# An FFN square and a gated residual computed in place in PSUM, and low words of weights stored one block earlier

## The chip, the core and the metric

The kernel runs on one core of a Trainium2 chip. Five engines matter: TensorE (PE in the profile, PEld for its weight loads), VectorE (DVE), ScalarE (ACT), GpSimd (POOL) and SyncE (SP), which only issues DMAs. The metric is the device time of one execution in microseconds; the kernel before takes 3242.33 us, the median of three runs (3240.86 to 3249.45).

## The reference

One layer of an encoder: 2048 prompt rows (16 tiles of 128) and 8 x 16 sample rows (one tile, SMP) go through a modulated norm, an input projection, two mixers (a gated delta rule and a band attention), an output projection with a gated residual, and an FFN with a squared relu and a second gated residual. The part that the change touches:

```python
    x = x + g1 * (jnp.concatenate([o_a, o_b], axis=-1) @ w_out)
    h = rmsnorm(x, norm2_g) * (1 + sc2) + sh2
    x = x + g2 * (jnp.square(jax.nn.relu(h @ w_up)) @ w_down)
```

Here w_out is 1024 x 1024, w_up 1024 x 4096 and w_down 4096 x 1024, all in float32.

## The kernel before

All large products are taken in three matmuls on split operands: an operand is rounded to a high word (type fp32r), and the remainder is a low word. `mm3` (L160) issues high x high, high x low and low x high into one PSUM accumulation.

Weights arrive in pieces of 128 x 1024 through `weights` (L166). SyncE loads the piece into a buffer `raw` (3 of them, `self.nraw`), ScalarE casts it into the high half of a buffer `w` (4 of them, `self.nw`), and the low half comes in one of two ways. If the low word of this piece was stored in DRAM earlier, SyncE loads it from there (L178). If not, GpSimd subtracts the high half from raw (L180) and, where `self.keep[name]` is set, SyncE stores the low half for later blocks (L183). All these DMAs stand in SyncE's one queue, in order.

Phase 1 (up to about 1127 us) is norm, input projection and the mixer of group A. Phase 2 goes over the blocks of tiles `BLOCKS2` = [0, 1], [2..5], [6..9], [10..13], [14, 15, SMP]. The text calls them blocks 0 to 4. For each block, `out_proj` (L1429) multiplies by w_out (8 pieces), applies gate and residual and prepares the norm, and `ffn` (L1492) multiplies by w_up (32 pieces, one `psu` each) and w_down (32 pieces). After each four rows of w_up, w_down's two halves follow for each tile (`psd`), and the next w_up piece is already issued in between. Attention for the next block is cut into steps and mixed into the FFN by a pace (`tick`). The final order of the instructions on each engine is the scheduler's, which runs when the program is built.

All of this shares one PSUM pool of `GP` = 3 banks (tag "g"): psu, psd, pso and the transposes for the norm. A bank comes free after the last reader. In `ffn_up` ScalarE writes the relu to `r` (one buffer) and its square, rounded, to the high word of `u`. VectorE squares r in place and subtracts the high word, which makes the low word of u. In `out_proj` VectorE writes the gated product to `gt` and adds it to `x1`. In block 0 the three weights are not kept, in block 1 all three are, and blocks 2 to 4 load all low words.

Of the kernel before, what the change touches and what calls it, by code (L numbers as in the profile page):

```python
# [8 lines left out]
F32 = mybir.dt.float32  # L9
F32R = mybir.dt.float32r  # L10
AF = mybir.ActivationFunctionType
ALU = mybir.AluOpType
AX = mybir.AxisListType.X

P = 128
# [36 lines left out]
class Trunk:  # L52
# [1376 lines left out]
    def out_proj(self, tiles, gates):  # L1429

        nc = self.nc
        x1 = []
        for j, t in enumerate(tiles):
            cs = slice(j * P, (j + 1) * P)
            for q, src in enumerate((self.s_oa, self.s_ob)):
                f = self.hp.tile([P, 4, P], F32, tag="htmp", name="of", bufs=2)
                nc.sync.dma_start(f, src[t])
                ks = slice(4 * q, 4 * q + 4)
                self.split(self.hT[:, ks, 0, cs], self.hT[:, ks, 1, cs], f)
        sts = [self.small.tile([P, 2, 6], F32, tag="bst", name="ost", bufs=NT2) for _ in tiles]  # L1440
        for group in ((0,), (1,), (2, 3)):
            wq = [self.wslices("w_out", 0, q * 256, 256, KT, 4) for q in group]
            for j, t in enumerate(tiles):
                if group[0] == 0:
                    x = self.fp.tile([P, D], F32, tag="x1", name="x1", bufs=self.nt)
                    nc.sync.dma_start(x, self.x_src(t))
                    x1.append(x)
                cs = slice(j * P, (j + 1) * P)
                for q, ws in zip(group, wq):
                    hs = slice(q * 256, (q + 1) * 256)  # L1450
                    ps = self.gp.tile([P, 512], F32, tag="g", name="pso")[:, 0:256]
                    for k in range(KT):
                        self.mm3(ps, self.hT[:, k, 0, cs], self.hT[:, k, 1, cs], ws[k][0], ws[k][1], k == 0, k == KT - 1)
                    tm = self.fp.tile([P, 256], F32, tag="gt", name="gt", bufs=2)
                    self.tt(tm, ps, gates[j][:, hs], ALU.mult)
                    self.tt(x1[j][:, hs], x1[j][:, hs], tm, ALU.add)
                    if q % 2:
                        nc.vector.bn_stats(sts[j][:, q // 2], x1[j][:, (q // 2) * 512:(q // 2 + 1) * 512])
                    self.tick(24 * 256)
                if group[-1] == 3:  # L1460
                    xn = self.normed(x1[j], t, sts[j])
                    self.later(lambda j=j, t=t, xn=xn: self.load_b(j, self.load_a(t, xn, 2, 3)), 3)
        return x1
# [6 lines left out]
    def ffn_up(self, fi, h2, T):  # L1470
        nc = self.nc
        mm = nc.tensor.matmul
        ws = self.wslices("w_up", 0, fi * P, P, KT, KT)
        ps = self.gp.tile([P, 512], F32, tag="g", name="psu")
        for c0, c1 in (((0, 256), (256, T)) if fi == 0 and T == 512 else ((0, T),)):
            if c1 == T:
                self.flush()
            for k in range(KT):
                wh, wl = ws[k]
                mm(ps[:, c0:c1], wh, h2[:, k, 0, c0:c1], start=(k == 0), stop=False)  # L1480
                mm(ps[:, c0:c1], wh, h2[:, k, 1, c0:c1], start=False, stop=False)  # L1481
                mm(ps[:, c0:c1], wl, h2[:, k, 0, c0:c1], start=False, stop=(k == KT - 1))  # L1482
        r = self.fp.tile([P, self.nt * P], F32, tag="r", name="r", bufs=1)
        self.act(r[:, 0:T], ps[:, 0:T], AF.Relu)
        u = self.fp.tile([P, 2, self.nt * P], F32R, tag="u", name="u", bufs=NGRP + 1)
        self.act(u[:, 0, 0:T], r[:, 0:T], AF.Square)
        self.tt(r[:, 0:T], r[:, 0:T], r[:, 0:T], ALU.mult)
        self.tt(u[:, 1, 0:T], r[:, 0:T], u[:, 0, 0:T].bitcast(F32), ALU.subtract)
        self.tick(24 * T)
        return u  # L1490

# [36 lines left out]
    def phase2(self):  # L1528
        nc, tc = self.nc, self.tc
        with ExitStack() as st:  # L1530
            P_ = lambda name, **kw: st.enter_context(tc.tile_pool(name=name, bufs=1, **kw))
            self.p2, self.hp, self.fp, self.sp = (P_(x) for x in ("p2c", "p2h", "p2f", "p2s"))
            self.nt = NT2
            self.xnp, self.xntag, self.nxn, self.inplace = self.fp, "y", self.nt, False
            self.hT = self.p2.tile([P, KT, 2, self.nt * P], F32R, name="hT2")
            for bi, tiles in enumerate(BLOCKS2):
                n = len(tiles)
                self.keep.update({k: bi == 1 for k in ("w_out", "w_up", "w_down")})
                gates = {t == SMP: None for t in tiles}
                for k in gates:  # L1540
                    gates[k] = self.gate_tile(0, k)
                x1 = self.out_proj(tiles, [gates[t == SMP] for t in tiles])
                if bi + 1 < len(BLOCKS2):
                    self.queue(*self.attention(BLOCKS2[bi + 1]))
                    if SMP in BLOCKS2[bi + 1]:
                        self.queue(self.sample_gen(), 2 + 9 * NB)
                    self.pace(0.95 * n * 24 * 2 * FF)
                self.ffn(tiles, self.hT, x1)
# [43 lines left out]
```

## Time and profile before

| what | value |
|---|---|
| median of three runs | 3242.33 us |
| profiled execution, its own time | 3235.24 us |
| its span from first to last instruction | 3233.5 us |
| PE busy | 3071.4 us, 95% of the span |
| VectorE, ScalarE, GpSimd busy | 59%, 46%, 22% |
| mean granted clock of TensorE | 0.977 |
| DMA | 730.71 MB, 226 GB/s over the span |

A matmul's end is modelled and matmuls overlap, so the busy time of PE says where it had work and not how fast it was. [...] By the instructions' tiles, the projection of block 0 begins at 1127 us and its FFN at 1187, the projection of block 1 at 1439 and its FFN at 1535, block 2 at 1941.

### The profile page before, as it was taken

Reading aid. Unit: us, or ns where it says so; the run is one execution under the profiler, and the core shown is the slowest. Engines: PE = TensorE matmul, PEld = TensorE weight load, DVE = VectorE, ACT = ScalarE, POOL = GpSimd, SP = SyncE. Lnnn points to the kernel's source line nnn. Section 1 sums busy time; section 2 is a strip of 40 time slices with the busy share of each in tenths; the row PEclk is TensorE's granted clock in tenths of the full one; section 3 lists DMA queues with packets and bytes.
Section 4 is the critical chain, followed back from the end, with each engine's and each line's share of the span. In section 5 each row is a group of like instructions: output and inputs, shape, how many; then the busy total and the mean of one; then the engine's idle time right before and its main releaser. Section 6 shows DMA issues by size and latency. Waiting matters only on the chain.

```text
span 3233.5 us, 53068 instructions
## 1 busy us (share of the span) xinstructions
PE 3071.4 (95%) x19577; PEld 2713.0 (84%) x19577; DVE 1903.2 (59%) x4526; ACT 1478.5 (46%) x2707; POOL 701.2 (22%) x561
## 2 busy tenths in 40 slices
PE   7899999999999979988999999999999999998998
PEld 6798988899989968878888889888888887787997
DVE  5985777777868676888446567235455443243223
ACT  3554544556656555554424444344434443333332
POOL 4641312121222347653343320000000000000000
PEclk9999999999989999998999999999999999998999
DMA  9789896878888765565565666665676667677875
GB/s 298 225 264 283 269 288 207 266 236 245 282 292 262 223 201 167 160 222 174 170 200 188 204 214 228 195 195 186 204 246 191 209 230 230 222 239 224 258 246 195
DMA packets 624507, 730.71 MB, mean 226 GB/s; under 512 B 59040, under 2 KB 483088, under 8 KB 622200
## 3 DMA queue, kind: packets, MB, share of 16 engines
q1 hardware_dynamic: 618488, 695.87, 68.0%
q0 software_dynamic: 5760, 31.46, 3.0%
q8 instruction: 154, 2.52, 0.3%
q14 instruction: 105, 0.86, 0.1%
HBM read 614.57 MB, written 115.52 MB: 226 GB/s over the span
## 4 chain that ended last, share of the span: by engine, by line
PE 71%; DVE 12%; DMA 9%; issue 3%; ACT 2%; SPq 1%; POOL 1%; POOLq 0%; DVEq 0%; ACTq 0%
PE psd L164 7%; PE psd L162 7%; PE psu L1480 7%; PE psu L1481 7%; PE psd L163 7%; PE psu L1482 7%; PE pv L1285 2%; PE psq L521 2%; PE psq L520 2%; PE psq L519 2%; PE psb L162 2%; PE psb L164 2%; PE psb L163 2%; PE psS L1267 2%; PE pso L162 2%
## 5 line engine op out<-in xcount | busy, mean ns | idle before, releaser
L175 ACT CAST w<-raw 128x1024 fp32r<-128x1024 f32 (+1 forms) x528 | 552.7, 1048 | 349.2 <-PE psd L164 163.2
L82 POOL TENSOR_TENSOR w<-raw,w 128x1024 fp32r<-128x1024 f32 (+1 forms) x172 | 418.3, 2443 | 365.8 <-ACT w L175 327.5
L1480 PE MATMUL psu<-hT,w 128*128 128x512 f32 (+2 forms) x1304 | 468.6, 361 | 7.1 <-ACT hT L104 6.2
L1481 PE MATMUL psu<-hT,w 128*128 128x512 f32 (+2 forms) x1304 | 467.2, 359 | 1.2 <-DVE hT L82 1.2
L1482 PE MATMUL psu<-hT,w 128*128 128x512 f32 (+2 forms) x1304 | 465.7, 357 | 0.0
L164 PE MATMUL psd<-w,u 128*128 128x512 f32 x1088 | 431.4, 398 | 9.1 <-DVE u L82 9.1
L162 PE MATMUL psd<-w,u 128*128 128x512 f32 x1088 | 432.5, 398 | 7.9 <-DVE y L82 4.1
L163 PE MATMUL psd<-w,u 128*128 128x512 f32 x1088 | 427.6, 393 | 0.0
L82 DVE TENSOR_TENSOR r<-r 128x512 f32<-128x512 f32 (+2 forms) x160 | 178.8, 1117 | 399.7 <-ACT u L92 399.4
L82 DVE TENSOR_TENSOR y<-y,psd 128x512 f32<-128x512 f32 x238 | 162.2, 684 | 242.0 <-PE psd L164 241.4
L1480 PEld LDWEIGHTS psu<-hT,w 128*128 128x128 f32 x1304 | 246.6, 190 | 39.8 <-ACT hT L104 7.4
L1481 PEld LDWEIGHTS psu<-hT,w 128*128 128x128 f32 x1304 | 246.8, 189 | 33.2 <-DVE hT L82 2.3
L1482 PEld LDWEIGHTS psu<-hT,w 128*128 128x128 f32 x1304 | 246.6, 189 | 32.5 <-issue 0.2
L92 ACT ACTIVATE r<-psu 128x512 f32<-128x512 f32 (+2 forms) x160 | 85.5, 534 | 408.7 <-PE psu L1482 349.6
L164 PEld LDWEIGHTS psd<-w,u 128*128 128x128 f32 x1088 | 204.9, 189 | 56.7 <-DVE u L82 10.4
L162 PEld LDWEIGHTS psd<-w,u 128*128 128x128 f32 x1088 | 205.3, 189 | 53.5 <-DVE y L82 6.7
L163 PEld LDWEIGHTS psd<-w,u 128*128 128x128 f32 x1088 | 205.6, 189 | 45.4 <-issue 1.0
L162 PE MATMUL psb<-w,hT 128*128 128x256 f32 x816 | 236.3, 290 | 0.7 <-ACT qraw L976 0.7
L164 PE MATMUL psb<-w,hT 128*128 128x256 f32 x816 | 234.1, 288 | 0.5 <-DVE hT L82 0.5
L163 PE MATMUL psb<-w,hT 128*128 128x256 f32 x816 | 233.4, 287 | 0.0
L520 PE MATMUL psq<-hT,w 128*128 128x384 f32 (+1 forms) x576 | 194.1, 337 | 0.0
L521 PE MATMUL psq<-hT,w 128*128 128x384 f32 (+1 forms) x576 | 193.9, 337 | 0.0
(318 smaller groups left out, 6603.0 us busy)
## 6 DMA issues: line engine op xcount, KB each, us to landing
raw<-in_w_up_dram SPq DMA_DIRECT2D x160, 512.0 KB
raw<-in_w_down_dram SPq DMA_DIRECT2D x160, 512.0 KB
raw<-in_w_in_dram SPq DMA_DIRECT2D x156, 512.0 KB
w<-s_w_in SPq DMA_DIRECT2D x130, 512.0 KB
w<-s_w_up SPq DMA_DIRECT2D x96, 512.0 KB
w<-s_w_down SPq DMA_DIRECT2D x96, 512.0 KB
raw<-in_w_out_dram SPq DMA_DIRECT2D x40, 512.0 KB
x<-in_x_prompt_dram SPq DMA_DIRECT2D x38, 512.0 KB
```

What stands on the lines that cost most here:

```text
L82: (eng or self.nc.vector).tensor_tensor(out, in0, in1, op)
L92: self.nc.scalar.activation(out, in_, func, **kw)
L162: mm(out, lh, rh, start=first, stop=False)
L163: mm(out, lh, rl, start=False, stop=False)
L164: mm(out, ll, rh, start=False, stop=last)
L175: nc.scalar.copy(w[:, 0, 0:n], r)
L519: mm(ps[:, 0:T], wh, hT[:, k, 0, 0:T], start=(k == 0), stop=False)
L520: mm(ps[:, 0:T], wh, hT[:, k, 1, 0:T], start=False, stop=False)
L521: mm(ps[:, 0:T], wl, hT[:, k, 0, 0:T], start=False, stop=(k == KT - 1))
L1480: mm(ps[:, c0:c1], wh, h2[:, k, 0, c0:c1], start=(k == 0), stop=False)
L1481: mm(ps[:, c0:c1], wh, h2[:, k, 1, c0:c1], start=False, stop=False)
L1482: mm(ps[:, c0:c1], wl, h2[:, k, 0, c0:c1], start=False, stop=(k == KT - 1))
```

## The change

There are three edits. In `out_proj` the product with the gate is written back into the PSUM bank and x1 is added from there; the buffer gt is gone. In `ffn_up` VectorE forms max(psu, 0) times r, which is the square, in the PSUM bank, and the low word is taken from the bank; r is no longer written by VectorE. In `phase2` the low words of w_out and w_down are made and stored in block 0 and loaded from block 1 on; those of w_up are made in blocks 0 and 1, stored in block 1 and loaded from block 2 on.

```diff
-                    tm = self.fp.tile([P, 256], F32, tag="gt", name="gt", bufs=2)
-                    self.tt(tm, ps, gates[j][:, hs], ALU.mult)
-                    self.tt(x1[j][:, hs], x1[j][:, hs], tm, ALU.add)
+                    self.tt(ps, ps, gates[j][:, hs], ALU.mult)
+                    self.tt(x1[j][:, hs], ps, x1[j][:, hs], ALU.add)
...
-        self.tt(r[:, 0:T], r[:, 0:T], r[:, 0:T], ALU.mult)
-        self.tt(u[:, 1, 0:T], r[:, 0:T], u[:, 0, 0:T].bitcast(F32), ALU.subtract)
+        self.stt(ps[:, 0:T], ps[:, 0:T], 0.0, r[:, 0:T], ALU.max, ALU.mult)
+        self.tt(u[:, 1, 0:T], ps[:, 0:T], u[:, 0, 0:T].bitcast(F32), ALU.subtract)
...
-                self.keep.update({k: bi == 1 for k in ("w_out", "w_up", "w_down")})
+                self.keep.update(w_out=bi == 0, w_up=bi == 1, w_down=bi == 0)
```

The scheduler also puts the instructions of phase 2 in another order; PE's order is the same up to the first projection of block 0. On VectorE, in the second group of w_up pieces of block 0's FFN (numbers tell the buffers apart: r and u are the relu and the two words of the square, psu the bank), there stood:

```order
L82 TENSOR_TENSOR r_15516<-r_15516 128x256
L82 TENSOR_TENSOR u_15518<-r_15516,u_15518 128x256
L82 TENSOR_TENSOR r_15562<-r_15562 128x256
L82 TENSOR_TENSOR u_15564<-r_15562,u_15564 128x256
L82 TENSOR_TENSOR r_15608<-r_15608 128x256
```

and now there stands:

```order
L79 SCALAR_TENSOR_TENSOR psu_15495<-psu_15495,r_15520 128x256
L82 TENSOR_TENSOR u_15522<-psu_15495,u_15522 128x256
L79 SCALAR_TENSOR_TENSOR psu_15541<-psu_15541,r_15566 128x256
L82 TENSOR_TENSOR u_15568<-psu_15541,u_15568 128x256
L79 SCALAR_TENSOR_TENSOR psu_15587<-psu_15587,r_15612 128x256
```

The number of VectorE's instructions is the same; both of each pair now read the bank, and only the first of them reads r.

On SyncE, at the first pieces of w_down in block 0 (raw and w are the buffers of a piece, s_w_down the stored low words, s_ob attention's output, q its queries), there stood:

```order
L174 DMA raw_15442<-in_w_down_dram 128x2x512
L174 DMA raw_15447<-in_w_down_dram 128x2x512
L1240 DMA q_16516<-s_q 128x128
L174 DMA raw_15487<-in_w_up_dram 128x8x128
L174 DMA raw_15533<-in_w_up_dram 128x8x128
```

and now there stands:

```order
L174 DMA raw_15444<-in_w_down_dram 128x2x512
L1292 DMA s_ob<-of_16025 64x128
L183 DMA s_w_down<-w_15391 128x1024
L174 DMA raw_15450<-in_w_down_dram 128x2x512
L1240 DMA q_16528<-s_q 128x128
L183 DMA s_w_down<-w_15397 128x1024
L174 DMA raw_15491<-in_w_up_dram 128x8x128
L183 DMA s_w_down<-w_15443 128x1024
L174 DMA raw_15537<-in_w_up_dram 128x8x128
```

Each store of a low word stands just ahead of the load of the raw piece that comes three pieces later, which takes the raw buffer of the piece stored.

## Rows read from the trace of the kernel before

**Rows 1.** Windows: stretch, length, busy us (instructions) per engine, clock, DMA share, GB/s
```profile
core 0: us, PE busy (x) PEld busy (x) DVE busy (x) ACT busy (x) POOL busy (x), PEclk, DMA share, GB/s
0.00:1120.00 1120.00, 1049.24 (x8241) 970.08 (x8242) 828.78 (x2482) 593.83 (x1238) 313.96 (x302) 0.97 0.83 260
...
1127.00:1187.00 60.00, 44.66 (x295) 40.34 (x296) 40.39 (x98) 30.03 (x58) 26.99 (x24) 0.86 0.71 232
1187.00:1439.00 252.00, 227.12 (x1467) 202.19 (x1466) 200.08 (x295) 137.99 (x252) 157.77 (x81) 0.98 0.56 169
1439.00:1535.00 96.00, 79.38 (x574) 75.64 (x573) 79.42 (x166) 42.86 (x82) 29.56 (x22) 0.86 0.61 197
1535.00:1941.00 406.00, 403.51 (x1960) 336.03 (x1958) 221.52 (x348) 167.05 (x274) 149.93 (x79) 1.00 0.61 195
1941.00:2413.00 472.00, 466.95 (x2480) 399.20 (x2481) 224.03 (x491) 202.74 (x336) 10.17 (x28) 1.00 0.63 205
```

**Rows 2.** Waits of PE in 1187:1439: us in total, times, longest us
```profile
PE psd L164 <- DVE u L82: 9.1, 3, 3.6
PE psd L162 <- ACT r L92: 3.7, 2, 2.6
PE psS L1267 <- DVE sm L1113: 2.8, 3, 1.2
...
PE psu L1480 <- ACT r L92: 0.9, 1, 0.9
```

**Rows 3.** Lines in 1187:1439: group xcount | busy us, mean ns | idle before, releasers
```profile
L82 POOL TENSOR_TENSOR w<-raw,w 128x1024 fp32r<-128x1024 f32 x63 | 154.8, 2472 | 76.9 <-ACT w L175 73.0 <-DMA raw<-in_w_out_dram 2.6 <-POOL bias L1235 0.8
L175 ACT CAST w<-raw 128x1024 fp32r<-128x1024 f32 x64 | 66.7, 1046 | 22.9 <-DMA raw<-in_w_down_dram 7.4 <-PE psd L164 7.1 <-DMA raw<-in_w_up_dram 3.0
L82 DVE TENSOR_TENSOR r<-r 128x256 f32<-128x256 f32 x32 | 51.5, 1609 | 29.5 <-ACT u L92 29.5
L82 DVE TENSOR_TENSOR u<-r,u 128x256 fp32r<-128x256 f32 x32 | 41.9, 1309 | 1.1
...
L92 ACT ACTIVATE u<-r 128x256 fp32r<-128x256 f32 x32 | 13.4, 418 | 0.3
L92 ACT ACTIVATE r<-psu 128x256 f32<-128x256 f32 x32 | 12.3, 385 | 50.4 <-DVE u L82 41.4 <-PE psu L1482 4.6 <-DVE sm L1116 4.2
```

**Rows 4.** Timeline in 1208:1214: start us, us, instruction, idle before and releaser
```profile
1205.71 4.87 POOL L82 TENSOR_TENSOR w<-raw,w 128x1024 fp32r<-128x1024 f32 x2 [3.08 <-ACT w L175]
1205.97 2.40 DVE L82 TENSOR_TENSOR r<-r 128x256 f32<-128x256 f32 x1 [0.44 <-ACT u L92]
...
1211.75 0.43 DVE L82 TENSOR_TENSOR r<-r 128x256 f32<-128x256 f32 x1 [0.90 <-ACT u L92]
```

**Rows 5.** Lines of VectorE in 1127:1187
```profile
L82 DVE TENSOR_TENSOR x<-x,gt 128x256 f32<-128x256 f32 x8 | 7.7, 983 | 0.1
L82 DVE TENSOR_TENSOR gt<-pso,gate 128x256 f32<-128x256 f32 x8 | 3.1, 414 | 0.7 <-PE pso L164 0.4 <-DMA x<-in_x_prompt_dram 0.3
```

**Rows 6.** Windows of PE alone: psu and psd of 512 columns, psu of 256
```profile
1550.00:1630.00 80.00, 80.00 (x350) 1.00 0.58 181
1225.00:1235.00 10.00, 10.00 (x86) 1.00 0.49 141
```

**Rows 7.** Waits of SyncE's queue in 1187:1439
```profile
SPq L174 <- POOL w L82: 90.2, 38, 5.6
```

**Rows 8.** Waits of PE in 1439:1535
```profile
PE pv L1285 <- DVE PT L82: 5.2, 2, 4.6
```

**Rows 9.** Lines in 1941:2413, block 2
```profile
L82 DVE TENSOR_TENSOR y<-y,psd 128x512 f32<-128x512 f32 x57 | 38.9, 686 | 59.0 <-PE psd L164 58.8
L82 DVE TENSOR_TENSOR r<-r 128x512 f32<-128x512 f32 x32 | 22.0, 688 | 89.3 <-ACT u L92 89.1
...
L92 ACT ACTIVATE r<-psu 128x512 f32<-128x512 f32 x32 | 19.2, 599 | 89.7 <-PE psu L1482 89.7
```

## The prediction

> **What bounds the kernel now.** I read the windows by stage first, since block by block the work differs. [rows 1] has PE busy for nearly all of each FFN stage from block 1 on: 403.5 of 406 us in 1535:1941, 467.0 of 472 in 1941:2413. There the matmuls set the time and an edit on VectorE can only cost. Three stretches are different: the projection of block 0 (1127:1187, PE idle 60 - 44.7 = 15.3 us), the FFN of block 0 (1187:1439, idle 252 - 227.1 = 24.9) and the projection of block 1 (1439:1535, idle 96 - 79.4 = 16.6). They are also where the granted clock is not full: 0.86, 0.98, 0.86. All that the change can give lies in these 408 us.
>
> Next, who is late there. In block 0's FFN the waits of PE [rows 2] name the square chain: psd on the low word u 9.1 us, psd on r 3.7 and psu on r 0.9, together 13.7 of 24.9; after that VectorE's softmax maximum with 2.8. Then why it is late [rows 3]: r times r takes 1609 ns on average for 256 columns and the low word 1309, and ScalarE's relu stood idle 41.4 us until VectorE had finished with the one buffer r. The timeline shows the reason [rows 4]: with GpSimd in two low words of weights (4.87 us in a row) r times r takes 2.40 us; a few microseconds later, the same shape takes 0.43. An operation that reads one operand from PSUM is not slowed beside the same GpSimd work: gt from pso and gate takes 414 ns in the stretch where x plus gt, both in SBUF, takes 983 [rows 5].
>
> **The change part by part.** *The square in the bank.* Both operations of the chain now have one operand in PSUM. A write of VectorE into PSUM stands nowhere in this trace, so I bound it: at best the 414 ns of [rows 5], at worst the 1609 ns of the operation that it replaces [rows 3]. I take 414, since the shape, the engine and the PSUM read are the same. Then VectorE loses 32 x (1.609 - 0.414) + 32 x (1.309 - 0.414) = 38 + 29 = 67 us of its 200 in block 0. The loop through r falls from 0.385 + 0.418 + 1.609 + 1.309 = 3.7 us to 0.385 + 0.418 = 0.8 us until r is free, since the square on ScalarE and the new multiply run side by side, and 1.2 us until u is done. One group of 24 matmuls of 256 columns takes 24 x 10.0/86 = 2.8 us [rows 6]: before, the loop was the slower of the two, afterwards it is not. So the 13.7 us go. [...] Of the 2.8 us on the softmax I give back 1.4, because VectorE goes from 79% to 53% busy.
>
> What is late next in block 0 is the supply of weights. A group of eight weights (four of w_up, four of w_down) needs 4 x 24 x 0.116 + 48 x 0.229 = 22 us of PE [rows 6] and 8 x 2.47 = 20 us of GpSimd [rows 3], which has 4 stages of w and 3 of raw to run ahead. ScalarE's cast already waited 7.4 + 3.0 us for raw weights. I charge 4 us for it. Sum in block 0's FFN: -13.7 - 4 - 1.4 + 4 = -15.
>
> *The gated residual in the bank.* It removes the buffer gt, and x1 is added from PSUM: in block 0 8 x (983 - 414) = 4.6 us of VectorE's 40, in a stretch where PE mostly waits for the first loads and for attention's chain. I count -2. The bank is held 0.4 us longer; three banks rotate, and PE's group is 2.8 us, so that is hidden.
>
> *Low words of w_out and w_down kept from block 0 on.* Block 0 gets 8 + 32 stores of 0.52 MB, 21 MB; block 1 loads them instead of making them. In block 0 the rate goes from 169 GB/s to about 169 + 17/0.252 = 236 in the FFN; the stretch 0:1120 ran at 260 [rows 1], so bandwidth does not run out, but a raw load takes longer; that is in the 4 us above. On SyncE each store waits for GpSimd's low word and is queued ahead of the next raw load. In the order, the store stands right before the raw load that reuses the very buffer which GpSimd's operation frees, and SyncE already waits there (90.2 us in 38 waits, [rows 7]); so the store adds its issue and no new wait, and only the loads of queries and bias rows and attention's stores behind it come later. In block 1, 40 of 72 operations of GpSimd vanish, 40 x 2.47 = 99 us, and the eight of w_out belong to 1439:1535. There VectorE is busy 79.4 of 96 us and the largest wait is PE's for attention's low words, 5.2 us [rows 8]. Without GpSimd beside it these operations go at their own pace. I count a good third of the 16.6 us, -6, and 3 of the up to 13 us that a clock of 0.86 costs (28% of 96 us at the lower level, half of it lost): -9. In 1535:1941 there are 2.5 us idle in all: -1.
>
> *What it costs.* The bank of psu was free after the relu, 0.60 us; now after relu, multiply and low word, 0.60 + 0.69 + 0.69 = 1.98 us for 512 columns [rows 9]. On the way from the fifth group of w_up to w_down the bank comes round after two groups of psd, 2 x 12 x 0.229 = 5.5 us. So 3.5 us of backlog on VectorE are covered in blocks 1 to 3, and PE has had hardly any wait there. Beyond that it is paid by PE. I charge +4 for blocks 1 to 4, together with what another order of the attention work may cost; the far end is in the rivals.
>
> What the profile of the same shape says of PSUM: y plus psd takes 686 ns and r times r in SBUF 688 [rows 9]. [...]
>
> **Sum.** -15 - 2 - 9 - 1 + 4 = -23 us. The profiled execution took 3235.2 us, 1.7 more than its span of 3233.5; so 3212 on its footing. The median of the three runs, 3242.3, is 7 us above the profiled one: 3242.3 - 23 = 3219 us.
>
> **Rivals.** First, the weights take the place of the chain: raw loads that compete with stores land later, the three raw buffers and four of w run dry in block 0, and PE waits for w where it waited for u. For it: 10.4 us of waits for raw in [rows 3] and GpSimd at 20 of 22 us per group. Against it: later groups of block 0 are stretched by attention, 252 us for 64 weights, 3.9 us each. Then block 0 keeps its time, the -2 and -9 - 1 shrink to -8 and +4 stays: 3238, no change. The same figure comes out if writing into PSUM costs what 1609 ns says, so that the change does not relieve VectorE.
>
> Second, slower: the banks. If VectorE's backlog at the switch from w_up to w_down exceeds 3.5 us, each further microsecond stops PE; there are eight switches in each block, 32 in blocks 1 to 4. At 1.4 us each, the added hold, it is 45 us, against -27 of gains: 3242 + 45 - 27 = 3260. It decides from 27/32 = 0.85 us a switch. For it: three banks for everything, and attention bursts on VectorE. Against it: VectorE is 47% busy in 1941:2413 and waits itself there [rows 1].
>
> Third, more: all waits of PE on VectorE in 1127:1535 go and the clock stays full: 13.7 + 2.8 + 5, two thirds of the 16.6 + 13 and half of the 15.3, 49 in all, less 4 of costs: 3242 - 45 = 3197.
>
> **How the numbers follow.** Forecast 0.56, no change through weights or a dear PSUM write 0.20, banks 0.10, more 0.14. Some 10 us, 0.3%, are about what a measurement of this kernel can tell from no change: faster means below 3232.6, slower above 3252. Nearly all of the forecast and of the third rival is faster, and a few parts of the first: 0.72. Same 0.17, slower 0.11. The range 3196 to 3246 takes in the third rival and the first, and leaves the bank case out.
>
> **What would show it.** Right: psu from psu and r, and u from psu, near 0.41 us at 256 columns with no long ones in blocks 0 and 1; no waits of psd on u or r in block 0; the relu's 41 us idle on u gone; block 0's FFN near 237 us, block 1's projection near 87; GpSimd some 99 us less in block 1. Wrong: waits of psd or psu on u in blocks 1 to 3 (banks), of PE on w or ScalarE on raw in block 0 (weights), a multiply well above 0.69 us at 512 columns (the PSUM write), or changed times in 0:1120, where no instruction moves.

## The result, and the profile after

With all three edits the kernel takes 3223.48 us (median of 5 runs, 3216.33 to 3228.73) against 3241.91 (median of 5, 3239.44 to 3249.45): 18.4 us less, a ratio of 0.994 with an interval of 0.9921 to 0.996. The profiled execution took 3216.33 us with a span of 3214.6.

The stages begin at the first matmul of pso or psu of a block, so block 1's FFN begins at 1528.6 us in the kernel before and not at 1535 as in [rows 1]. The time up to the first pso is left out: it differed between the profiled executions, one of each kernel, by up to 12 us (1126.3 to 1138.5). The recorded instructions stand in the same order there up to 1113 us, and one and the same matmul shortly behind that started between 1114.4 and 1126.6. In us:

| kernel | block 0 projection | block 0 FFN | block 1 | blocks 2 to 4 | sum |
|---|---|---|---|---|---|
| before | 60.1 | 251.4 | 502.2 | 1292.6 | 2106.3 |
| all three edits | 66.1 | 226.3 | 501.8 | 1294.0 | 2088.2 |

So the gain is the FFN of block 0, 25 us, of which the projection ahead of it gives back 6. Block 1 gained nothing. Blocks 2 to 4 take 1292.6 to 1300.8 us in the twelve kernels of this document, so a difference of a few microseconds in a stage of a single profile says little.

The windows of the kernel after answer to [rows 1] (same columns):

```profile
1126.00:1192.00 66.00, 45.61 (x287) 41.06 (x288) 39.66 (x93) 29.33 (x56) 27.25 (x24) 0.80 0.78 262
1192.00:1419.00 227.00, 221.15 (x1475) 200.39 (x1474) 149.79 (x299) 139.53 (x252) 149.62 (x79) 1.00 0.82 258
1419.00:1508.00 89.00, 76.03 (x548) 72.79 (x547) 63.37 (x153) 39.41 (x75) 10.80 (x12) 0.85 0.58 190
1508.00:1921.00 413.00, 408.54 (x1982) 339.25 (x1981) 186.62 (x364) 170.42 (x279) 76.21 (x51) 1.00 0.62 199
```

In the second row PE idles 5.9 us instead of 24.9, VectorE is busy 149.8 us instead of 200.1, the clock is full (1.00 instead of 0.98), and DMA moves 258 GB/s instead of 169. In the first row PE idles 20.4 us instead of 15.3 and the clock is 0.80.

The lines of that FFN answer to [rows 3] (group, count, busy us, mean ns, idle before):

```profile
L82 POOL TENSOR_TENSOR w<-raw,w 128x1024 fp32r<-128x1024 f32 x60 | 144.2, 2411 | 54.8 <-ACT w L175 48.2 <-DMA raw<-in_w_up_dram 5.7 <-POOL bias L1235 0.3
L175 ACT CAST w<-raw 128x1024 fp32r<-128x1024 f32 x63 | 65.9, 1047 | 50.8 <-DMA raw<-in_w_down_dram 17.6 <-DMA raw<-in_w_up_dram 16.9 <-PE psd L164 8.5
...
L79 DVE SCALAR_TENSOR_TENSOR psu<-psu,r 128x256 f32<-128x256 f32 x32 | 13.5, 423 | 10.7 <-ACT r L92 10.7
L82 DVE TENSOR_TENSOR u<-psu,u 128x256 fp32r<-128x256 f32 x32 | 13.5, 422 | 22.4 <-ACT u L92 21.4
...
L92 ACT ACTIVATE r<-psu 128x256 f32<-128x256 f32 x32 | 12.3, 383 | 10.9 <-PE psu L1481 5.3 <-DVE psu L79 5.2
```

The multiply takes 423 ns and the low word 422, where they took 1609 and 1309, and the relu waits 5.2 us for VectorE instead of 41.4. The price of the stores is in the second row: the cast waits 34.5 us for raw weights instead of 10.4 (5.8 in the run e1 below, which has the square and not the stores). Little of it reaches PE, as the waits of PE in the same window show, which answer to [rows 2]:

```profile
PE pv L1285 <- DVE PT L82: 1.5, 1, 1.5
...
PE psd L162 <- DVE u L82: 0.7, 2, 0.5
PE psu L1481 <- POOL w L82: 0.6, 1, 0.6
```

VectorE's other work did not get shorter. More of what is left in SBUF now falls beside GpSimd's subtractions. In the kernel before, the scaling of the softmax took (window 1187:1439)

```profile
L87 DVE TENSOR_SCALAR sS<-sS,sm 128x640 f32<-128x640 f32 x12 | 8.6, 720 | 0.4
...
L87 DVE TENSOR_SCALAR sS<-sS,sm 128x384 f32<-128x384 f32 x6 | 2.5, 416 | 0.1
```

and in the kernel after (window 1192:1419)

```profile
L87 DVE TENSOR_SCALAR sS<-sS,sm 128x640 f32<-128x640 f32 x12 | 14.4, 1197 | 0.4
...
L87 DVE TENSOR_SCALAR sS<-sS,sm 128x384 f32<-128x384 f32 x6 | 8.3, 1379 | 0.1
```

By the starts and ends in the traces, 7 of the 12 larger scalings overlap a subtraction of GpSimd after the change and take 1659 ns on average, the other 5 take 550; before it 2 of 12 overlapped one (1554 ns), and the other 10 took 554.

In the run e8 below, in which GpSimd writes zeros instead of subtracting, the larger scaling takes 561 ns on average.

### The profile page after: what moved, and what is told of

Same layout as the page of the kernel before. It is cut to its first block, busy times and chain, and to the rows that moved or that the text cites. A ratio compares the mean times of both kernels' runs of the same rounds, so it can differ in the third digit from the quotient of the medians.

```text
span 3214.6 us, 53090 instructions
## 1 busy us (share of the span) xinstructions
PE 3059.3 (95%) x19577; PEld 2704.5 (84%) x19577; DVE 1805.8 (56%) x4526; ACT 1479.9 (46%) x2707; POOL 599.3 (19%) x521
## 4 chain that ended last, share of the span: by engine, by line
PE 70%; DMA 13%; DVE 11%; issue 2%; ACT 2%; POOL 2%; SPq 1%; ACTq 0%; POOLq 0%; DVEq 0%
PE psu L1479 7%; PE psd L164 7%; PE psd L162 7%; PE psu L1480 7%; PE psu L1481 7%; PE psd L163 7%; DMA x<-in_x_prompt_dram 2%; PE psb L163 2%; PE psb L162 2%; PE psb L164 2%; PE psq L520 1%; PE psq L521 1%; PE psq L519 1%; PE psS L1267 1%; PE pv L1285 1%
## 5 line engine op out<-in xcount | busy, mean ns | idle before, releaser
L82 POOL TENSOR_TENSOR w<-raw,w 128x1024 fp32r<-128x1024 f32 (+1 forms) x132 | 317.6, 2415 | 301.5 <-ACT w L175 232.4
L79 DVE SCALAR_TENSOR_TENSOR psu<-psu,r 128x512 f32<-128x512 f32 (+2 forms) x160 | 98.8, 617 | 417.0 <-ACT r L92 417.0
## 6 DMA issues: line engine op xcount, KB each, us to landing
raw<-in_w_up_dram SPq DMA_DIRECT2D x160, 512.0 KB
raw<-in_w_down_dram SPq DMA_DIRECT2D x160, 512.0 KB
raw<-in_w_in_dram SPq DMA_DIRECT2D x156, 512.0 KB
w<-s_w_in SPq DMA_DIRECT2D x130, 512.0 KB
w<-s_w_down SPq DMA_DIRECT2D x128, 512.0 KB
w<-s_w_up SPq DMA_DIRECT2D x96, 512.0 KB
raw<-in_w_out_dram SPq DMA_DIRECT2D x40, 512.0 KB
x<-in_x_prompt_dram SPq DMA_DIRECT2D x38, 512.0 KB
```

The lines of the kernel that those rows point to most:

```text
L79: (eng or self.nc.vector).scalar_tensor_tensor(out, in0, scalar, in1, op0, op1)
L82: (eng or self.nc.vector).tensor_tensor(out, in0, in1, op)
```

## The experiments

The ten experiments in us, by stage as above, with the median of the timed runs and its ratio to the runs of the kernel before beside them:

| run | edits | projection 0 | FFN 0 | block 1 | blocks 2 to 4 | median | ratio (interval) |
|---|---|---|---|---|---|---|---|
| e1_square | square | 60.8 | 218.4 | 503.1 | 1296.0 | 3209.29 | 0.989 (0.9877 to 0.9903) |
| e2_residual | residual | 61.4 | 249.7 | 500.8 | 1295.4 | 3238.51 | 0.9977 (0.9964 to 0.9991) |
| e3_keep | earlier stores | 70.1 | 244.5 | 501.1 | 1295.9 | 3244.46 | 1.0002 (0.9989 to 1.0014) |
| e4_square_keep | square, stores | 70.3 | 223.7 | 505.5 | 1299.2 | 3226.04 | 0.9944 (0.9926 to 0.9961) |
| e5_square_down | square, w_down's stores | 63.1 | 220.0 | 501.2 | 1297.3 | 3218.87 | 0.9922 (0.9904 to 0.994) |
| e6_square_keep_poolq | e4, other queue | 65.7 | 227.2 | 502.3 | 1300.8 | 3225.74 | 0.9936 (0.9912 to 0.9959) |
| e7_square_residual | square, residual | 62.0 | 222.5 | 503.3 | 1293.6 | 3210.5 | 0.9897 (0.988 to 0.9913) |
| e8_no_subtract | before, zeros in block 0 | 55.2 | 218.3 | 512.0 | 1296.6 | 3215.52 | 0.9916 (0.9897 to 0.9936) |
| e9_square_to_sbuf | multiply only reads PSUM | 62.7 | 227.2 | 505.2 | 1296.1 | 3225.7 | 0.9939 (0.9917 to 0.9961) |
| e10_square_all_in_0 | square, 72 stores | 70.6 | 231.8 | 487.0 | 1299.6 | 3226.0 | 0.9939 (0.9916 to 0.9962) |

**Each edit alone.** Each experiment keeps some of these pairs of lines and leaves the others as before:

```diff
# e1, e4 (square)
-        self.tt(r[:, 0:T], r[:, 0:T], r[:, 0:T], ALU.mult)
-        self.tt(u[:, 1, 0:T], r[:, 0:T], u[:, 0, 0:T].bitcast(F32), ALU.subtract)
+        self.stt(ps[:, 0:T], ps[:, 0:T], 0.0, r[:, 0:T], ALU.max, ALU.mult)
+        self.tt(u[:, 1, 0:T], ps[:, 0:T], u[:, 0, 0:T].bitcast(F32), ALU.subtract)
# e2 (residual)
-                    self.tt(tm, ps, gates[j][:, hs], ALU.mult)
-                    self.tt(x1[j][:, hs], x1[j][:, hs], tm, ALU.add)
+                    self.tt(ps, ps, gates[j][:, hs], ALU.mult)
+                    self.tt(x1[j][:, hs], ps, x1[j][:, hs], ALU.add)
# e3, e4 (stores)
-                self.keep.update({k: bi == 1 for k in ("w_out", "w_up", "w_down")})
+                self.keep.update(w_out=bi == 0, w_up=bi == 1, w_down=bi == 0)
```

> Only the FFN square and its low word are taken from the PSUM bank; the residual and the block in which low words are stored stay as before. Theory (the square chain beside GpSimd was what stopped PE in block 0): block 0's FFN, 252 us before, takes 225 to 232, the projection of block 0 stays at 60 us and of block 1 at 90, and the time falls by 20 to 26 us, so more than with all three edits (18 us). Rival (the scheduler's new order or the earlier stores make the gain): block 0's FFN stays above 245 us and the time within 8 us of before.

Measured: 3209.29 us, 36.6 below before and some 14 below all three edits; the intervals of the two ratios do not touch. The gain is larger than I expected, and it lies where the theory put it. The stages show 28 us of it (a sum of 2078.3 against 2106.3): the profiled execution of before, at 3235.24 us, lay 7 to 11 us below the medians of its runs. Up to block 0's FFN e1 has PE's order of before, and in that FFN as many matmuls of attention (308), so the gain is not work that went elsewhere. Block 0's FFN in e1 (columns as in [rows 1]) and the one wait of PE in it:

```profile
1192.00:1410.00 218.00, 216.52 (x1459) 198.31 (x1459) 146.23 (x290) 137.13 (x250) 155.07 (x81) 1.00 0.61 185
PE pv L1285 <- ACT Q L1252: 1.5, 1, 1.5
```

PE idles 1.5 us in 218. So GpSimd, busy 155 of 218 us, supplies the weights in time; the weights do not take the place of the chain.

> Only the gated residual is computed in the bank. Theory: no gain, 0 to +6 us, with new waits of pso on the add of x1 (DVE x) at each projection, 1 to 3 us each, since the bank is held until x1 and VectorE's second operation are there. Rival (the prediction's term): -2 us, and no waits of pso on x.

Measured: 7 us faster, so both theories missed. The waits of pso on x are there (2.6 us in 2 waits), but they are shorter than those on gt before (4.9 in 3). The stages show none of the 7 us (2107.4 against 2106.3, the latter from the execution below its median), so where it comes from stays open.

> Only the low words of w_out and w_down are stored in block 0 and loaded from block 1 on. Theory: no gain by itself. The projection of block 0 grows from 60 to some 66 us because the loads of q stand behind stores on SyncE; block 0's FFN is the same or up to 6 us longer; block 1 is 0 to 4 us shorter; together -2 to +10 us. Rival (GpSimd's relief in block 1 is worth 9 us, as predicted): block 1's projection falls from 90 to 81 us and the time by 5 to 10.

Measured: no change of time, as the theory has it, though its stages cancel differently: block 0's projection 10 us longer, its FFN 7 shorter. In that FFN PE idles 16.5 us instead of 24.9, and the multiply and the low word take 1523 and 1175 ns instead of 1609 and 1309; why is not shown, and the order of attention's work is another there. The rival is partly right: block 1's projection falls from 89.9 to 83.0 us (85.7 in e4). But 137 matmuls of attention (pq, psS, psP and pv) fall into it instead of 151, the FFN behind it takes 418.1 instead of 412.3, and block 1 as a whole gains 1 us.

> The square in the bank and the earlier stores, without the residual in the bank. Theory: the waits of pso on x are gone, block 0's FFN is 225 to 230 us, block 0's projection 64 to 67, and the time is 20 to 26 us below before. Rival (the residual in the bank is harmless or helps): the time is the same as with all three edits, 16 to 20 us below before.

Measured: 3226.04 us, the same as with all three edits, as the rival had it. The residual in the bank is not what holds the kernel after back. Against e1 the stores cost 9.5 us in the projection and 5.3 in the FFN of block 0.

The square and the residual together, with the stores as before, are e7 (the two pairs of lines of e1 and e2):

> The square and the residual in the bank, the low words stored as before. Theory (the earlier stores are what costs, the residual in the bank gives a little): 3200 to 3211 us, the fastest so far. Rival (the residual's longer hold of the bank costs once GpSimd is out of the way): 3212 to 3222 us, with waits of pso on x of 8 us and more in all.

Measured: 3210.5 us, a ratio of 0.9897 (0.988 to 0.9913), the same as the square alone. pso waits for x 2.6 us in 2 waits (first line), where it is 9.5 us in 6 with all three edits (second line):

```profile
PE pso L162 <- DVE x L82: 2.6, 2, 2.3
PE pso L162 <- DVE x L82: 9.5, 6, 2.7
```

So those longer waits of the kernel after come with the stores.

**What the stores cost.** In e5 only w_down's low words are kept from block 0 on. In e6 all are, but issued from GpSimd's queue. In e10 w_up's are stored in block 0 as well:

```diff
# e5, on e1
+                self.keep.update(w_out=bi == 1, w_up=bi == 1, w_down=bi == 0)
# e6, on e4
-            nc.sync.dma_start(kept[m][:, 0:n], w.bitcast(F32)[:, 1, 0:n])
+            (nc.sync if name == "w_in" else nc.gpsimd).dma_start(kept[m][:, 0:n], w.bitcast(F32)[:, 1, 0:n])
# e10, on e1
+                self.keep.update({k: bi == 0 for k in ("w_out", "w_up", "w_down")})
```

> The square in the bank; low words of w_down stored in block 0, those of w_out and w_up in block 1 (the residual as before). Theory (the eight stores of w_out fall into the first 20 us of block 0's projection, where the DMA engines are already full): that projection is back at 60 to 62 us, against 70 with all three low words of w_out stored there, and block 0's FFN keeps its 222 to 226 us; the time is 3212 to 3222. Rival (the stores as a whole cost, wherever they stand): the projection stays at 66 us or more.

> The square in the bank and the earlier stores, but the stores of low words in the FFN weights and w_out are issued by GpSimd, which makes them, so that SyncE's queue has none of them. Theory (the DMA engines are full there): block 0's projection stays at 65 us or more. Rival (the stores hold up the loads of q behind them in SyncE's queue): it falls to 60 to 62 us.

Without the eight stores of w_out the projection is at 63.1 us, 7 below e4 and 2 above e1; the 32 stores of w_down cost its FFN 1.6 us. In the medians e5 is still 9.6 us above e1, while its stages add up to 3 more (2081.5 against 2078.3), so w_down's stores cost something as well, and where is not shown. Moved to the other queue, the stores of e6 leave the projection at 65.7: over the 65 of the theory, but 4.6 below e4. That does not show a part of SyncE's queue: 64 matmuls of attention fall into the projection of e6 and 94 into that of e4, and pso waits 8.3 us for gt in e6, so the run does not part the two. What DMA does in those microseconds is in the windows, which begin with the first pso of each run. Before:

```profile
1127.20:1147.20 20.00, 13.91 (x84) 11.92 (x84) 6.46 (x14) 7.53 (x13) 9.89 (x13) 0.81 1.00 352
1147.20:1167.20 20.00, 18.15 (x142) 17.71 (x142) 15.14 (x28) 10.34 (x16) 12.94 (x6) 0.93 0.74 227
```

With the square and the stores (e4):

```profile
1133.40:1153.40 20.00, 12.78 (x78) 11.29 (x78) 8.02 (x8) 5.92 (x9) 9.66 (x13) 0.79 1.06 375
1153.40:1173.40 20.00, 16.47 (x103) 15.40 (x104) 10.58 (x25) 6.24 (x11) 5.92 (x3) 0.70 0.89 307
```

The DMA engines were full in the first 20 us already (share 1.00, 352 GB/s); the stores make the next 20 us nearly full too (0.89, 307 GB/s against 0.74, 227), and PE loses work (16.5 us busy against 18.2) and clock (0.70 against 0.93) there. The three runs with the stores and the old residual (e3, e4, e10) have this projection at 70.1 to 70.6 us, the four without w_out's stores that keep before's order there (before, e1, e5, e9) at 60.1 to 63.1. PE is held there by attention's queries: in e4 ScalarE waits 3.5 us for a load of q, and PE 7.6 us for the qs made from it, against nothing and 1.3 us in e1. The order of attention's work is a little different in the three, and no run has the stores in the old order; e2 and e7, without them and in another order again, are at 61.4 and 62.0.

> The square in the bank, and the low words of all three weights stored in block 0, 72 stores instead of 40; from block 1 on GpSimd makes none. Theory (the stores fill DMA in block 0, and GpSimd's relief in block 1 is worth little): block 0's projection 66 to 72 us and its FFN 224 to 232 (218 without stores, 224 with 40), block 1 in all 496 to 508 us as before; the time 3218 to 3238. Rival (block 1 gains from a free GpSimd, as predicted with 9 us): block 1 falls below 494 us and the time below 3215.

In e10, and below the dots block 1 in e1:

```profile
1209.00:1441.00 232.00, 224.99 (x1503) 204.30 (x1502) 153.02 (x317) 145.08 (x263) 150.36 (x81) 0.99 0.96 317
1441.00:1520.50 79.50, 71.67 (x563) 68.63 (x563) 61.49 (x156) 40.88 (x76) 2.99 (x9) 0.96 0.69 222
1520.50:1928.00 407.50, 402.49 (x1927) 334.20 (x1926) 166.97 (x339) 164.50 (x265) 6.02 (x20) 1.00 0.62 201
...
1410.00:1500.00 90.00, 74.47 (x553) 71.14 (x551) 73.37 (x152) 38.98 (x75) 25.80 (x18) 0.89 0.59 194
1500.00:1913.00 413.00, 408.62 (x1974) 339.76 (x1975) 192.99 (x366) 170.59 (x279) 153.43 (x83) 1.00 0.62 200
```

Here each side had a part. Block 1 does fall, to 487 us from 503 in e1, as the rival said: with GpSimd at 3 us in its projection that takes 79.6 us, PE idles 7.8 and the clock is 0.96. But block 0 pays 9.8 us in the projection and 13.4 in the FFN (DMA share 0.96), so the time is that of e4. More than half of block 1's fall is work that moved: 347 matmuls of attention stand in block 0's FFN instead of 308 and 510 in block 1 instead of 551, so PE is busy 8.5 us more in the first and 9 us less in the second. What is left for block 1 is 7 us less of idle PE and a higher clock in the projection; what is left as the price in block 0's FFN is some 5 us.

**Why the square was slow.**

```diff
# e8, on before: blk0 is set in block 0
-        self.tt(w[:, 1, 0:n], r, w[:, 0, 0:n].bitcast(F32), ALU.subtract, eng=nc.gpsimd)
+        if self.blk0:
+            nc.gpsimd.memset(w[:, 1, 0:n].bitcast(F32), 0.0)
+        else:
+            self.tt(w[:, 1, 0:n], r, w[:, 0, 0:n].bitcast(F32), ALU.subtract, eng=nc.gpsimd)
# e9, on before
-        self.tt(r[:, 0:T], r[:, 0:T], r[:, 0:T], ALU.mult)
+        self.stt(r[:, 0:T], ps[:, 0:T], 0.0, r[:, 0:T], ALU.max, ALU.mult)
```

> The kernel before, but in block 0 GpSimd writes zeros as the low words of weights instead of reading raw and w and subtracting, so block 0's products lack the low word of the weights. Nothing is changed in the square. Theory (r times r and the low word of u are slow because GpSimd reads SBUF at the same time): both fall to 0.41 to 0.5 us at 256 columns and block 0's FFN to 215 to 230 us from 252. Rival (the square is slow or late for its own chain through the one buffer r): they stay above 1 us on average and the FFN above 240 us.

```profile
L181 POOL MEMSET w<- 128x1024 f32 x60 | 57.6, 960 | 124.0 <-PE psd L164 56.7 <-PE psu L1485 55.6 <-ACT Q L1255 4.3
L82 DVE TENSOR_TENSOR r<-r 128x256 f32<-128x256 f32 x32 | 13.6, 425 | 43.9 <-ACT u L92 43.9
L82 DVE TENSOR_TENSOR u<-r,u 128x256 fp32r<-128x256 f32 x32 | 13.5, 422 | 1.1
...
L87 DVE TENSOR_SCALAR sS<-sS,sm 128x640 f32<-128x640 f32 x12 | 6.7, 561 | 0.4
```

The square of before, with nothing in PSUM, takes 425 and 422 ns once GpSimd only writes, and block 0's FFN takes 218.3 us, as in e1. (That it agrees to 0.1 us is chance: attention's work lies differently, with 61 of its matmuls in the projection instead of 89, 319 in the FFN instead of 308 and 572 in block 1 instead of 551; the shorter projection and the longer block 1 of e8 go with that.)

GpSimd is also busy for less time here, so the means alone do not say what held VectorE up. The single instructions do. In the kernel before, 23 of the 32 multiplies overlap a subtraction of GpSimd and take 2075 ns on average, the other nine 420; of the low words 16 overlap one and take 2197, the other 16 take 422. In e1, with one operand in the bank, 20 and 27 overlap one and take 427 and 423. And in e8 three multiplies, four low words and twelve of attention's operations on SBUF (of from otmp) overlap a memset; they take 422, 425 and 277 ns, as the others do. So the square was slow where it ran beside GpSimd's subtraction, which reads SBUF (2075 and 2197 ns), and not beside the memset, which does not (422 and 425), and the bank is a way around it (427 and 423).

> Only the multiply of the square reads the PSUM bank; it writes its product to r in SBUF, and the low word of u is taken from r as before. So the multiply has one operand in SBUF, the low word still two, and the bank is held through the multiply alone. Theory (an operation with two SBUF operands is slow beside GpSimd, one with a PSUM operand is not): the multiply takes 0.41 to 0.43 us, the low word 1.2 us or more, the loop through r 0.385 + 0.418 + 0.42 + 1.3 = 2.5 us just under PE's 2.8; block 0's FFN 222 to 240 us, the time 3212 to 3230. Rival (a write into the bank is needed too, or the low word alone decides): above 243 us in block 0's FFN. Rival (the shorter hold of the bank gains): below 3205 us.

```profile
L82 DVE TENSOR_TENSOR u<-r,u 128x256 fp32r<-128x256 f32 x32 | 38.6, 1206 | 1.1
L79 DVE SCALAR_TENSOR_TENSOR r<-psu,r 128x256 f32<-128x256 f32 x32 | 13.4, 420 | 40.9 <-ACT u L92 40.9
```

As expected: the operation with a PSUM operand takes 420 ns, the one with two operands in SBUF 1206, in the same stretch. FFN 0 is at 227.2 us, so the multiply is worth 24 us and the low word 9 more. In blocks 2 to 4, where GpSimd makes no low words, e9 takes 1296.1 us and e1, which holds the bank longer, 1296.0: there the shorter hold gains nothing.

## Why the prediction was right

The time came out at 3223 where 3219 was forecast, inside the range. But three terms of the sum were off, and their errors nearly cancelled; that the time came so near is in part luck.

- *The chain in block 0's FFN, -15: right in mechanism, too small.* It was 25 us of gain with all edits and 33 with the square alone. I counted 13.7 us of waits on u and r, 4 for the clock and half of the softmax waits, and charged 4 for weights. No run shows the 4 for the clock, nor the 5 that the third rival has for it: they were my estimate from the 0.98 of [rows 1], which is 2% short of full over 252 us, 5 us at most; what the runs show is 1.00 in this stage, with all edits and in e1. In e1 PE's idle time fell from 24.9 to 1.5 us: the other 11 us, of which 6 were attention's waits on VectorE, went nearly whole as well, where I had counted 1.4. VectorE has 54 us less to do (200.1 to 146.2), and the clock is full (1.00). Of the rest, some 5 us beyond idle time and clock, I cannot say where it came from. With the square alone no wait of PE for weights is left in the records.
- *The earlier stores, "bandwidth does not run out": this step failed.* I set the average of the FFN, 236 GB/s, against an average of 260 in phase 1, and did not look at the 20 us in which the stores of w_out fall. DMA was full there before (share 1.00, 352 GB/s). The projection, forecast 2 us shorter, is 6 longer; e4 against e1, and e5, show that w_out's eight stores are the larger part of that. In the FFN the cast waits 24 us more for raw weights than before, and PE idles 4 us more than in e1 (5.9 against 1.5), which is what I had charged for it.
- *Block 1, -9 and -1: failed.* GpSimd lost the work that I counted (76 of 150 us are left in its FFN), but the projection of block 1 took 89 us as before, with a largest wait of 3.7 us, of pv on VectorE. With the stores and the old residual (e3, e4) it falls to 83.0 and 85.7, and the FFN behind it gives that back; in e10, where GpSimd makes no low words at all in block 1, it falls to 79.6, but over half of block 1's gain there is work moved to block 0. So some 7 us of relief is the most that a run shows, and half the relief gave block 1 as a whole nothing. The clock of 0.86 in that projection, 1439 to 1535 us, is a mean: by windows of 2 us in the kernel before it reads 0.50 from 1447 to 1463 us and from 1527 to 1535, and 1.00 in nearly all the rest. No run shows apart the 3 us that I counted for it; in the kernel after it is 0.85.
- *The residual, -2, with a hold "that is hidden":* alone it gave 7 us, which no stage shows, and on top of the square nothing (e7 against e1). The hold is not hidden everywhere: with all three edits pso waits 9.5 us for x in 6 waits.
- *The banks, +4: nothing that the runs can tell.* Blocks 2 to 4 take 1292.6 us before and 1294.0 after; the other runs that keep the old square or hold the bank only through the multiply (e2, e3, e8, e9) take 1295.4 to 1296.6 there. In blocks 1 to 3 of the kernel after no wait of psd or psu on u is in the records. The rival is out.
- *The PSUM write at 414 ns:* 423. At 512 columns the multiply takes 700 ns and the low word 687 in block 2 (first two lines, of the kernel after), against 688 [rows 9] and 685 before (last line):

```profile
L79 DVE SCALAR_TENSOR_TENSOR psu<-psu,r 128x512 f32<-128x512 f32 x32 | 22.4, 700 | 111.4 <-ACT r L92 111.4
L82 DVE TENSOR_TENSOR u<-psu,u 128x512 fp32r<-128x512 f32 x32 | 22.0, 687 | 13.8 <-ACT u L92 13.6
L82 DVE TENSOR_TENSOR u<-r,u 128x512 fp32r<-128x512 f32 x32 | 21.9, 685 | 0.8
```

So with both ends of the operation in PSUM the multiply takes 12 ns more than in SBUF at 512 columns, and at 256 columns 2 ns less (423 against the 425 of e8).

The fastest version is the square alone, 3209.29 us, 0.4% below all three edits; with the residual (e7, 3210.5 us) it is the same.

## What to carry to other kernels

When VectorE's operations on SBUF vary at one shape as they do here (420 to 2075 ns), look at what GpSimd does at that moment, and give each of them one operand in PSUM; here the bank's longer hold cost nothing that could be measured (1296.0 us in blocks 2 to 4 in e1, 1296.1 in e9). Price added DMA traffic in the 20 us in which it falls (a share of 1.00 here), not by the average of a stage (0.71). Take an edit of several parts apart even if the whole gains: here the stores gave back nearly half of what the square had won (17 of 37 us, e4 against e1). And before a stage is compared between two runs, count what work stands in it: the scheduler moved attention's matmuls between stages, and in e6 and e10 that was as large as the effect sought.

## What the runs showed of the hardware

VectorE writes a result into the bank that it reads at nearly the pace of SBUF without GpSimd beside it: 423 ns for 256 columns against 425 in e8, 700 for 512 against 688 [rows 9]. The scaling of the softmax, with one full operand in SBUF (sS<-sS,sm), is held up beside GpSimd's subtraction as well: in the kernel after, 1659 ns for those of 640 columns that overlap one against 550 for the others. And with the instructions in the same order, the time to one and the same matmul varied from 1114.4 to 1126.6 us between the profiled executions, one of each kernel, so that stages say more than spans of single profiles.
